# A Conformer and gMLP layer on one core: every third low half of the weights on GpSimd

## The chip, the cores and the metric

The kernel runs on one core of a Trainium2 chip. The metric is the time of one execution on the device in microseconds (us). The engines are named as in the profile: PE is TensorE (matmuls), DVE is VectorE, ACT is ScalarE, POOL is GpSimd, SP issues most of the DMAs. Each engine works through its own list of instructions in order, and semaphores make one wait for another.

## The reference

One layer works on 512 tokens of 1024 channels, in float32:

```python
h = h + 0.5 * swiglu(rms_norm(h, ffn1_norm), ffn1_w_gu, ffn1_w_down)      # 1024 -> 2 x 2816 -> 1024
n = rms_norm(h, mix_norm)
a_val, a_gate, b_u, b_v, g_a, g_b = split(n @ w_in + b_in, 6)             # 1024 -> 6 x 1024
y_a = silu(layer_norm(causal_depthwise_conv(a_val * sigmoid(a_gate)))) @ w_a_out   # width 31
y_b = (gelu(b_u) * spatial_mix(layer_norm(gelu(b_v)))) @ w_b_out          # chunks of 128 tokens
h = h + (sigmoid(g_a) * y_a + sigmoid(g_b) * y_b) @ w_out
h = h + memory_cross_attention(rms_norm(h), rms_norm(mem), w_q, w_kv, w_o)  # 4 heads, 256 tokens
h = h + 0.5 * swiglu(rms_norm(h, ffn2_norm), ffn2_w_gu, ffn2_w_down)
y = rms_norm(h, final_norm)
```

## The kernel before

The activations lie transposed, channels on 128 partitions and the 512 tokens along the free axis, in eight tiles. Every large product is done in three passes of TensorE on numbers split in two: the high half is the number rounded to the engine's fast float32 form (fp32r), the low half what is left. `mm3` adds high x high, high x low and low x high into one PSUM tile.

Weights come in blocks of up to 128 x 1024 numbers. `wfetch` loads a block (four buffers, DMAs issued by SP), `wsplit` makes its halves: ScalarE writes the high half (`whi`, line 96), VectorE subtracts it from the raw block and writes the low half (`wlo`, line 97); each half has three buffers. A block then feeds 24 matmuls of 512 columns. A block's split can start only when the buffers of the block three before it have been read by TensorE.

The stages are: the first feed-forward (pairs `g`, `u`, then `d`), keys of the memory (`pk`), the input projection (`av`, `ag`, then `r` with tokens on partitions, then `gb`), the branch B product (`yb`), gates A (`ga`), values (`pv`), branch A (`ya`), the output product (`o`), attention (`pq`, `wo`), and the second feed-forward. The name of a low half in the profile is that of its product, the first K tile of the block and an l: `gb0w0l`.

The convolution is vector work: 240 steps (line 344), each multiplies a shifted channel tile by a weight and adds it. They run at any time after their channel tile exists and are written as generators; `spend` issues some of them behind each block of weights, by assumed lengths (a split 1.14 us, a K tile's matmuls 0.65 us). When all of a tile's steps are done it is added to `csum` (line 348), whose mean is a matmul, `pmean` (line 501). On top of this order of writing, the framework's scheduler sets the final list of each engine: it runs a model of the engines' timeline and picks, among the instructions that are ready there, by the order of writing. So a change of one instruction's engine changes the lists of all engines.

GpSimd has little to do: constants at the start, the powers -1/2 of the norms (`pow_mhalf`, line 196), one mask (line 369), and the issue of the loads of a few rows (lines 366 and 376). VectorE's other work in the convolution's stretch are evictions of `r` (line 387, from PSUM), the layer norm of branch B (lines 401 to 413) and halves of activations (line 180).

Of the kernel before, what the change touches and what calls it, by code (L numbers as in the profile page):

```python
# [10 lines left out]
F32 = mybir.dt.float32  # L11
F32R = mybir.dt.float32r
AF = mybir.ActivationFunctionType
ALU = mybir.AluOpType
# [11 lines left out]
CW = 31  # L26
# [6 lines left out]

# lengths that the order of issue goes by: a K tile's products of 512 columns, a block's split, a vector operation
MM_US, SPLIT_US, OP_US = 0.65, 1.14, 0.66
# [12 lines left out]
def conformer_layer(ctx: ExitStack, tc: tile.TileContext, xT, memT, vecs, rows, w_gu1, w_dn1, w_in_f, w_in_t,  # L48
# [33 lines left out]
    def wfetch(srcs, name):  # L82
        """the blocks [128, K tiles, 128 or 512 columns] one after the other in one tile"""
        raw = wpool.tile([P, 1024], F32, tag="raw", name=name, bufs=4)
        n = 0
        for src in srcs:
            m = src.shape[1] * src.shape[2]
            nc.sync.dma_start(out=raw[:, n:n + m], in_=src.rearrange("p k c -> p (k c)"))
            n += m
        return raw[:, :n]  # L90

    def wsplit(raw, c, name):
        n = raw.shape[1]
        hi = wpool.tile([P, 1024], F32R, tag="whi", name=name + "h", bufs=3)[:, :n]
        lo = wpool.tile([P, 1024], F32R, tag="wlo", name=name + "l", bufs=3)[:, :n]
        S.copy(out=hi, in_=raw)  # L96
        V.tensor_tensor(out=lo, in0=raw, in1=hi.bitcast(F32), op=ALU.subtract)  # L97
        return hi.rearrange("p (k c) -> p k c", c=c), lo.rearrange("p (k c) -> p k c", c=c)
# [8 lines left out]

    # steps of vector work that may run at any time (generators that give each step's length) stand behind the
    # blocks of weights, as many as the products of a block leave room for; soon: in order, first; later: by turns
    soon, later = deque(), deque()  # L110
    room = [None]

    def spend(us):
        """vector work us long has been issued; positive room is filled with steps"""
        if room[0] is not None:
            room[0] = min(room[0], 4.0) - us
            while (soon or later) and room[0] > 0:
                steps = soon or later
                used = next(steps[0], None)
                if used is None:  # L120
                    steps.popleft()
                    continue
                room[0] -= used
                if steps is later and len(steps) > 1:
                    steps[0], steps[1] = steps[1], steps[0]
# [9 lines left out]
    def part(acc, wsrc, ahi, alo, k0, k1, name):  # L135
        """K tiles k0 to k1 of a product with wsrc [128, K tiles, 128 columns] stationary, activations moving."""
        nk = wsrc.shape[1]
        whi, wlo = wload(wsrc[:, k0:k1, :], f"{name}w{k0}")
        for k in range(k0, k1):
            mm3(acc, whi[:, k - k0, :], wlo[:, k - k0, :], ahi[k], alo[k], k == 0, k == nk - 1)  # L140
        spend(SPLIT_US - MM_US * (k1 - k0) * acc.shape[1] / T)

    def linear(wsrc, ahi, alo, name, n=T):
        """a whole product: PSUM tile [128 columns, n]"""
        nk = wsrc.shape[1]
        acc = new_ps(name)[:, :n]
        for k0 in range(0, nk, 8):
            part(acc, wsrc, ahi, alo, k0, min(nk, k0 + 8), name)
        return acc

    def linear_pair(wsrcs, ahi, alo, name):
        """two products side by side, K tile by K tile, for activations that come one by one"""
        accs = [new_ps(f"{name}{i}") for i in range(2)]
        for k0 in range(0, DT, DT // 2):
            ks = slice(k0, k0 + DT // 2)
            whi, wlo = wsplit(wfetch([w[:, ks, :] for w in wsrcs], f"{name}w{k0}"), P, f"{name}w{k0}")
            for k in range(k0, k0 + DT // 2):
                for i in range(2):
                    c = i * DT // 2 + k - k0
                    mm3(accs[i], whi[:, c, :], wlo[:, c, :], ahi[k], alo[k], k == 0, k == DT - 1)  # L160
        return accs

    def linear_rows(wsrc, ahi, alo, ntok, name):
        """activations stationary, wsrc [128, K tiles, 512 columns] moving: PSUM tiles [128 tokens, 512]."""
        nk = wsrc.shape[1]
# [33 lines left out]
    def rstat(accs, n, eps, name, copy=True):  # L199
        """accs [128, n]: per partition sums of squares. 1/sqrt(mean + eps) as columns [128 tokens, n/128] and as  # L200
        rows on all partitions [128, n]."""
        nt = n // P
# [21 lines left out]
    def prep(m, g, acc):  # L224
        """residual tile m is final: operands of the next product and its part of the norm."""
        split_x(m, g)
        add_square(acc, h[:, m, :], m == 0)
# [23 lines left out]
    def ffn_up(w_gu, rb, first=()):  # L251
        """the hidden activations, split; first: products of the first pairs that are already there"""
        f = [gate_up(pg, pu, rb, j) for j, (pg, pu) in enumerate(first)]
# [8 lines left out]

    # the first two pairs of products go along with the loads, K tile by K tile
    HF = DT // 2
# [70 lines left out]
    def conv(i):  # L335
        """causal depthwise convolution of a channel tile; tap k reaches CW - 1 - k tokens back"""
        c = slot(f"cv{i}")
# [12 lines left out]

    # gated channels
    room[0] = 0
# [10 lines left out]

    # spatial gating unit, tokens on partitions
    wsr = slot("wsr")
    nc.gpsimd.dma_start(out=wsr, in_=sgu_wT.rearrange("s g t -> s (g t)"))
    # [s, t]: kept where t >= s
    wsr3 = wsr.rearrange("s (g t) -> s g t", g=GROUPS)
# [10 lines left out]
    def token_major(which):  # L379
        """gelu of 1024 columns of the input projection: tiles [token tile][column half]"""  # L380
        out = [[None, None] for _ in range(TT)]
# [68 lines left out]

    # the rest of the keys and the values of the memory, and the steps of the spatial gating in between
    vts = [[None, None], [None, None]]
# [30 lines left out]

    # sigmoid(gate_B) * y_B
    for m in range(DT):
# [12 lines left out]

    # layer norm over channels, swish
    pmean = ps2.tile([P, T], F32, tag="st", name="pmean")  # L500
# [24 lines left out]

    # sigmoid(gate_A) * y_A, merge
    mgh, mgl = [], []
# [44 lines left out]
    def softmax(hd):  # L572
        """probabilities [128 tokens, memory], two token tiles side by side"""
        out = []
# [53 lines left out]

    # independent products stand between the steps of a head
    q = {}  # L630
# [28 lines left out]
    for m in range(last):  # L659
        add_half(m, linear(w_dn2[m], fh, fl, f"d{m}"))  # L660
        add_square(acc, h[:, m, :], m == 0)
        S.activation(h[:, m, :], h[:, m, :], AF.Copy, scale=col("final_norm", m))
    # the last product and the final norm by halves of the tokens
    ws = [wload(w_dn2[last][:, k0:min(FT, k0 + 8), :], f"dl{k0}") for k0 in range(0, FT, 8)]
# [76 lines left out]
```

## Time and profile before

| | us |
|---|---|
| time, median of 3 runs (lowest, highest) | 1356.83 (1355.51, 1357.62) |
| span of the profiled execution | 1355.1 |
| PE busy | 1332.3 |
| DVE busy | 777.9 |
| ACT busy | 456.5 |
| POOL busy | 19.4 |

The profile is of one execution; its span runs from the first instruction to the last, and its whole time is not given apart from the span. Busy time is the time in which an engine has an instruction at work. Instructions of one engine overlap a little at their ends: a matmul of 512 columns is recorded with 0.40 us though the next starts 0.23 us later, and two VectorE operations overlap by some 0.08 us. The start and end of GpSimd's instructions are rough.

### The profile page before, as it was taken

How to read it: one execution, taken by the hardware profiler on the slowest of the kernel's cores; microseconds unless marked ns; L12 is line 12 of the kernel's file. 1: busy time of each engine (PE TensorE's matmuls, PEld its weight loads, DVE VectorE, ACT ScalarE, POOL GpSimd, SP SyncE). 2: the span in 40 equal slices, each digit the busy share in tenths (PEclk: the TensorE clock that was granted, in tenths of full speed). 3: DMA queues.
4: the chain of work that ended last, by engine and by line, in shares of the span. 5: the costliest groups of instructions: out<-in, count | busy, mean ns of one | idle time of the engine just before them, and what ended most of it. 6: DMA issues, size and time to landing. Idle time of an engine off the chain costs nothing.

```text
span 1355.1 us, 14923 instructions
## 1 busy us (share of the span) xinstructions
PE 1332.3 (98%) x5968; PEld 1079.1 (80%) x5968; DVE 777.9 (57%) x1078; ACT 456.5 (34%) x618; POOL 19.4 (1%) x31
## 2 busy tenths in 40 slices
PE   7999999999999999999999999999999999999996
PEld 6788888888898888888787788887878888888886
DVE  5544444434367999998996775554644444442323
ACT  5322222223233223343224743334432222222221
POOL 0000000000020000100000000000000000000000
PEclk9999999999999999999999999999999999999998
DMA  6333333233353332322233333202332333323321
GB/s 207 109 94 93 94 93 94 86 96 109 114 181 115 94 94 94 101 97 76 92 94 116 102 109 109 62 20 76 123 93 93 94 94 93 94 86 101 86 70 62
DMA packets 40660, 132.47 MB, mean 98 GB/s; under 512 B 4432, under 2 KB 7248, under 8 KB 40592
## 3 DMA queue, kind: packets, MB, share of 16 engines
q1 hardware_dynamic: 39872, 129.17, 30.9%
q0 software_dynamic: 720, 2.36, 0.6%
q8 instruction: 46, 0.75, 0.2%
q14 instruction: 22, 0.18, 0.0%
HBM read 129.42 MB, written 2.10 MB: 97 GB/s over the span
## 4 chain that ended last, share of the span: by engine, by line
PE 97%; DVE 1%; ACT 1%; DMA 0%; issue 0%; SPq 0%; DVEq 0%; POOLq 0%; ACTq 0%
PE u L106 6%; PE g L104 6%; PE u L105 6%; PE g L105 6%; PE g L106 6%; PE u L104 6%; PE d L106 6%; PE d L104 6%; PE d L105 6%; PE r L173 2%; PE r L172 2%; PE r L174 2%; PE ya L104 1%; PE ya L105 1%; PE o L105 1%; PE av L105 1%
## 5 line engine op out<-in xcount | busy, mean ns | idle before, releaser
L344 DVE SCALAR_TENSOR_TENSOR cv<-ap,vec,cv 128x494 f32<-128x494 f32 (+24 forms) x240 | 163.3, 729 | 0.4
L244 DVE TENSOR_TENSOR u<-u,n4rb 128x512 f32<-128x512 f32 x22 | 15.2, 692 | 70.3 <-PE u L106 70.3
L244 DVE TENSOR_TENSOR u<-u,n1rb 128x512 f32<-128x512 f32 x20 | 13.8, 691 | 65.8 <-PE u L106 65.8
L240 DVE TENSOR_TENSOR g<-g,n4rb 128x512 f32<-128x512 f32 x22 | 15.2, 692 | 51.7 <-PE g L106 47.5
L240 DVE TENSOR_TENSOR g<-g,n1rb 128x512 f32<-128x512 f32 x20 | 13.8, 691 | 43.3 <-PE g L106 43.3
L246 DVE TENSOR_TENSOR f<-s,u 128x512 f32<-128x512 f32 x44 | 30.4, 692 | 5.4 <-ACT s L242 1.1
L261 DVE SCALAR_TENSOR_TENSOR h<-d,h 128x512 f32<-128x512 f32 x15 | 10.4, 692 | 31.5 <-PE d L106 31.5
L242 ACT ACTIVATE s<-g 128x512 f32<-128x512 f32 x44 | 27.8, 633 | 0.1
L192 DVE TENSOR_TENSOR acc<-acc,sq 128x512 f32<-128x512 f32 x34 | 23.3, 685 | 0.1
L191 ACT ACTIVATE sq<-h 128x512 f32<-128x512 f32 x34 | 21.2, 624 | 1.4 <-DVE h L261 0.2
L184 DVE SCALAR_TENSOR_TENSOR xlo<-h,vec,xhi 128x512 fp32r<-128x512 f32 x24 | 17.7, 746 | 5.3 <-ACT xhi L183 5.2
L183 ACT ACTIVATE xhi<-h,vec 128x512 fp32r<-128x512 f32 x24 | 17.2, 717 | 1.9 <-DVE h L626 1.0
L543 DVE TENSOR_TENSOR h<-o,h 128x512 f32<-128x512 f32 x8 | 5.5, 692 | 13.7 <-PE o L106 13.7
L532 DVE TENSOR_TENSOR ga<-ya,sga 128x512 f32<-128x512 f32 x8 | 5.5, 690 | 13.4 <-PE ya L106 13.4
L387 DVE TENSOR_TENSOR uv<-r,br 128x512 f32<-128x512 f32 x16 | 10.7, 686 | 0.1
L104 PE MATMUL fg<-xhi,first0h 128*128 128x512 f32 x4 | 2.2, 553 | 7.8 <-ACT first0h L96 7.8
L587 ACT ACTIVATE pr<-sc,mx 128x256 f32<-128x256 f32 x16 | 7.4, 470 | 6.4 <-DVE mx L584 6.3
L567 DVE TENSOR_TENSOR qt<-pq,n3rb 128x512 f32<-128x512 f32 x8 | 5.3, 687 | 7.3 <-ACT n3rb L218 4.3
L626 DVE TENSOR_TENSOR h<-wo,h 128x512 f32<-128x512 f32 x8 | 5.4, 688 | 7.0 <-PE wo L106 7.0
L388 ACT ACTIVATE uv<-uv 128x512 f32<-128x512 f32 x16 | 9.0, 621 | 0.6 <-DVE uv L387 0.6
L583 DVE TENSOR_REDUCE mx<-sc 128x2 f32<-128x512 f32 x8 | 5.5, 692 | 3.7 <-PE sc L106 3.3
L97 DVE TENSOR_TENSOR d1w8l<-d1w,d1w8h 128x1024 fp32r<-128x1024 f32 x2 | 2.5, 1226 | 8.7 <-ACT d1w8h L96 8.7
(4300 smaller groups left out, 4279.4 us busy)
## 6 DMA issues: line engine op xcount, KB each, us to landing
h<-xT SPq DMA_DIRECT2D x8, 256.0 KB, 5.9
first<-w_gu SPq DMA_DIRECT2D x8, 256.0 KB, 6.1
d0w<-w_dn SPq DMA_DIRECT2D x4, 512.0 KB, 3.5
d1w<-w_dn SPq DMA_DIRECT2D x4, 512.0 KB, 3.7
d2w<-w_dn SPq DMA_DIRECT2D x4, 512.0 KB, 3.4
d3w<-w_dn SPq DMA_DIRECT2D x4, 512.0 KB, 3.5
d4w<-w_dn SPq DMA_DIRECT2D x4, 512.0 KB, 3.6
d5w<-w_dn SPq DMA_DIRECT2D x4, 512.0 KB, 3.4
```

Of the source, the lines that this page charges most:

```text
L104: PE.matmul(out, whi, ahi, start=start, stop=False)
L105: PE.matmul(out, whi, alo, start=False, stop=False)
L106: PE.matmul(out, wlo, ahi, start=False, stop=stop)
L172: PE.matmul(accs[t], a_h, whi[:, k - k0, :], start=k == 0, stop=False)
L173: PE.matmul(accs[t], a_h, wlo[:, k - k0, :], start=False, stop=False)
L174: PE.matmul(accs[t], a_l, whi[:, k - k0, :], start=False, stop=k == nk - 1)
L192: V.tensor_tensor(out=acc, in0=acc, in1=sq, op=ALU.add)
L240: V.tensor_tensor(out=g1, in0=pg, in1=rb, op=ALU.mult)
L242: S.activation(s1, g1, AF.Silu)
L244: V.tensor_tensor(out=u1, in0=pu, in1=rb, op=ALU.mult)
L246: V.tensor_tensor(out=f, in0=s1, in1=u1, op=ALU.mult)
L344: V.scalar_tensor_tensor(out=o, in0=aps[i][:, :T - back], scalar=w, in1=o, op0=ALU.mult, op1=ALU.add)
```

## The change

Every third call of `wsplit` gives the subtract to GpSimd instead of VectorE. The rest of the diff removes comments and blank lines, with no effect on the program; lines from 95 on stand three further down.

```diff
+    turn = [0]
+
     def wsplit(raw, c, name):
         n = raw.shape[1]
         hi = wpool.tile([P, 1024], F32R, tag="whi", name=name + "h", bufs=3)[:, :n]
         lo = wpool.tile([P, 1024], F32R, tag="wlo", name=name + "l", bufs=3)[:, :n]
         S.copy(out=hi, in_=raw)
-        V.tensor_tensor(out=lo, in0=raw, in1=hi.bitcast(F32), op=ALU.subtract)
+        turn[0] += 1
+        (G if turn[0] % 3 == 0 else V).tensor_tensor(out=lo, in0=raw, in1=hi.bitcast(F32), op=ALU.subtract)
```

GpSimd's list, from the second norm's power (n2r) to the loads of the rows for the `r` products. Before:

```order
L196 TENSOR_TENSOR nmr<-nmm,mhalf 128x2
L196 TENSOR_TENSOR n2r<-n2m,mhalf 128x4
L366 DMA wsr<-sgu_wT 128x512
L369 AFFINE_SELECT wsr<-wsr 128x512
L376 DMA br_3436<-rows 128x512
L376 DMA br_3599<-rows 128x512
```

The same place in the changed kernel:

```order
L199 TENSOR_TENSOR n2r<-n2m,mhalf 128x4
L100 TENSOR_TENSOR av0w0l<-av0w_2809,av0w0h 128x1024
L100 TENSOR_TENSOR ag1w0l<-ag1w_2920,ag1w0h 128x1024
L100 TENSOR_TENSOR av3w0l<-av3w_3040,av3w0h 128x1024
L100 TENSOR_TENSOR ag4w0l<-ag4w_3155,ag4w0h 128x1024
L100 TENSOR_TENSOR av6w0l<-av6w_3273,av6w0h 128x1024
L100 TENSOR_TENSOR ag7w0l<-ag7w_3387,ag7w0h 128x1024
L100 TENSOR_TENSOR r10w4l<-r10w_3513,r10w4h 128x1024
L369 DMA wsr<-sgu_wT 128x512
L372 AFFINE_SELECT wsr<-wsr 128x512
L379 DMA br_3436<-rows 128x512
L100 TENSOR_TENSOR r11w2l<-r11w_3637,r11w2h 128x1024
```

The loads of the mask's weights and of the bias rows, which stood right behind n2r, now stand behind seven subtracts and more.

VectorE's list where it comes to the low half gb0w0l (cv are convolution steps; the columns tell how far each channel tile has come, a smaller number being a later step). Before:

```order
L97 TENSOR_TENSOR pk7w0l<-pk7w_4164,pk7w0h 128x1024
L344 SCALAR_TENSOR_TENSOR cv_3418<-ap_3114,vec,cv_3418 128x492
L344 SCALAR_TENSOR_TENSOR cv_3583<-ap_3193,vec,cv_3583 128x493
L387 TENSOR_TENSOR uv_4101<-r_3948,br_3946 128x512
L344 SCALAR_TENSOR_TENSOR cv_4095<-ap_3270,vec,cv_4095 128x508
L387 TENSOR_TENSOR uv_4104<-r_3949,br_3946 128x512
L387 TENSOR_TENSOR uv_4107<-r_3950,br_3946 128x512
L387 TENSOR_TENSOR uv_4110<-r_3951,br_3946 128x512
L344 SCALAR_TENSOR_TENSOR cv_3418<-ap_3114,vec,cv_3418 128x491
L344 SCALAR_TENSOR_TENSOR cv_3583<-ap_3193,vec,cv_3583 128x492
L97 TENSOR_TENSOR gb0w0l<-gb0w_4209,gb0w0h 128x1024
```

The same place in the changed kernel:

```order
L347 SCALAR_TENSOR_TENSOR cv_4095<-ap_3270,vec,cv_4095 128x507
L347 SCALAR_TENSOR_TENSOR cv_3583<-ap_3193,vec,cv_3583 128x487
L390 TENSOR_TENSOR uv_4101<-r_3948,br_3946 128x512
L347 SCALAR_TENSOR_TENSOR cv_3418<-ap_3114,vec,cv_3418 128x482
L390 TENSOR_TENSOR uv_4104<-r_3949,br_3946 128x512
L347 SCALAR_TENSOR_TENSOR cv_4095<-ap_3270,vec,cv_4095 128x506
L390 TENSOR_TENSOR uv_4107<-r_3950,br_3946 128x512
L347 SCALAR_TENSOR_TENSOR cv_3583<-ap_3193,vec,cv_3583 128x486
L390 TENSOR_TENSOR uv_4110<-r_3951,br_3946 128x512
L351 TENSOR_TENSOR csum<-csum,cv_3418 128x512
L100 TENSOR_TENSOR gb0w0l<-gb0w_4209,gb0w0h 128x1024
```

pk7w0l has gone to GpSimd, and by gb0w0l the channel tile cv_3418 has come to its last step (482 columns) and its csum, where it stood at 491 before. From av2w0l to gb0w0l VectorE's list held 30 low halves, 135 convolution steps and 2 csum before, and holds 20, 152 and 3 now. From gb0w0l to the last csum it held 21 low halves, 105 steps and 5 csum, and holds 13, 88 and 4. In TensorE's list pmean stands 62 matmuls earlier than before, and near av2 the order of two blocks is changed: before, the block ag1 is read in one piece ahead of av2's low half; now TensorE reads av2w0l first, where it read ag1w0l, and ag1w0l seven matmuls later.

## Rows read from the trace of the kernel before

**Rows 1.** The page's first part: busy us (share of the span) xinstructions.
```profile
span 1355.1 us, 14923 instructions
...
PE 1332.3 (98%) x5968; PEld 1079.1 (80%) x5968; DVE 777.9 (57%) x1078; ACT 456.5 (34%) x618; POOL 19.4 (1%) x31
```

**Rows 2.** Waits of PE: waiting, released by, us in total, times, longest.
```profile
PE fg L104 <- ACT first0h L96: 7.8, 1, 7.8
...
PE po L104 <- ACT ph L179: 2.3, 4, 0.6
...
PE ya L104 <- ACT aa0h L179: 1.3, 1, 1.3
PE yb L104 <- ACT yb5w0h L96: 0.2, 1, 0.2
```

**Rows 3.** Busy us by stretch, each with its number of instructions, and the clock.
```profile
core 0: us, PE busy (x) PEld busy (x) DVE busy (x) ACT busy (x) POOL busy (x), PEclk, DMA share, GB/s
50.00:380.00 330.00, 330.00 (x1416) 265.49 (x1415) 137.00 (x167) 95.61 (x123) 0.00 (x0) 1.00 0.32 97
419.40:584.10 164.70, 164.70 (x724) 133.19 (x723) 156.26 (x225) 50.78 (x62) 4.27 (x5) 1.00 0.32 101
584.10:708.70 124.60, 124.01 (x578) 100.57 (x578) 117.75 (x173) 39.81 (x54) 0.00 (x0) 1.00 0.29 93
```

**Rows 4.** Timeline of DVE: start us, us, engine line op out<-in xcount, idle before.
```profile
649.70 6.56 DVE L344 SCALAR_TENSOR_TENSOR cv<-ap,vec,cv 128x488 f32<-128x488 f32 x10
...
661.05 1.22 DVE L97 TENSOR_TENSOR yb4w0l<-yb4w,yb4w0h 128x1024 fp32r<-128x1024 f32 x1
662.18 1.22 DVE L97 TENSOR_TENSOR yb5w0l<-yb5w,yb5w0h 128x1024 fp32r<-128x1024 f32 x1
```

**Rows 5.** Timeline of POOL.
```profile
1.37 0.29 POOL masks.py:199 TENSOR_SCALAR_AFFINE_SELECT ident<-ident 128x128 f32<-128x128 f32 x1
...
389.22 2.07 POOL L196 TENSOR_TENSOR n2r<-n2m,mhalf 128x4 f32<-128x4 f32 x1 [6.02 <-DVE n2m L208]
...
395.20 0.64 POOL L369 TENSOR_SCALAR_AFFINE_SELECT wsr<-wsr 128x512 f32<-128x512 f32 x1 [3.23 <-DMA wsr<-sgu_wT]
...
857.69 1.01 POOL L196 TENSOR_TENSOR n3r<-n3m,mhalf 128x4 f32<-128x4 f32 x1 [121.64 <-DVE n3m L208]
```

**Rows 6.** DVE beside them; then line 329: ns min/median/max, first and last start.
```profile
389.20 1.23 DVE L97 TENSOR_TENSOR pk4w0l<-pk4w,pk4w0h 128x1024 fp32r<-128x1024 f32 x1
...
395.40 0.98 DVE L329 SCALAR_TENSOR_TENSOR xn<-h,vec,n2rb 128x512 f32<-128x512 f32 x1 [1.29 <-ACT n2rb L218]
...
L329 DVE SCALAR_TENSOR_TENSOR xn<-h,vec,n2rb x8: 737/741/981, 395.4 to 407.7; 128x512 f32<-128x512 f32 x8
```

**Rows 7.** Timelines of ACT, DVE and PE at the blocks ag1 and av2.
```profile
415.94 1.05 ACT L96 CAST ag1w0h<-ag1w 128x1024 fp32r<-128x1024 f32 x1 [6.85 <-PE av L105]
416.90 1.05 ACT L96 CAST av2w0h<-av2w 128x1024 fp32r<-128x1024 f32 x1
...
418.17 1.22 DVE L97 TENSOR_TENSOR av2w0l<-av2w,av2w0h 128x1024 fp32r<-128x1024 f32 x1
...
418.73 0.40 PE L106 MATMUL ag<-xhi,ag1w0l 128*128 128x512 f32 x1
```

**Rows 8.** Timelines of DVE and PE at gb0.
```profile
582.86 1.22 DVE L97 TENSOR_TENSOR gb0w0l<-gb0w,gb0w0h 128x1024 fp32r<-128x1024 f32 x1
...
587.04 0.40 PE L106 MATMUL gb<-xhi,gb0w0l 128*128 128x512 f32 x1
```

**Rows 9.** Timelines of DVE and PE at the last csum and at pmean.
```profile
708.00 0.69 DVE L348 TENSOR_TENSOR csum<-csum,cv 128x512 f32<-128x512 f32 x1
...
713.76 1.02 PE L501 MATMUL pmean<-csum,avg 128*128 128x512 f32 x2
```

**Rows 10.** Timelines of DVE and PE at a block of the first feed-forward.
```profile
47.42 1.22 DVE L97 TENSOR_TENSOR g4w0l<-g4w,g4w0h 128x1024 fp32r<-128x1024 f32 x1
...
57.14 0.40 PE L106 MATMUL g<-xhi,g4w0l 128*128 128x512 f32 x1
```

## The prediction

> **What bounds the kernel now.** I read the page's first part, then the waits of TensorE, then the busy time of the engines by stretch, and last the timelines of VectorE and GpSimd in the stretch where VectorE is full. The reader is to see first that TensorE is busy for 1332.3 of 1355.1 us, VectorE for 777.9 and GpSimd for 19.4 [rows 1]. Of TensorE's idle time 7.8 us lie at the start and the rest mostly at the end; the waits in between are a few us in all, such as 2.3 us for the softmax's halves and 1.3 us for the first normed channel tile [rows 2]. So a shorter VectorE can bring almost nothing, 4 us at most: 22.8 us of idle less the start and some 11 us of the end. What can go wrong is that TensorE starts to wait.
>
> VectorE's share of 57% is an average over two kinds of stage. In the feed-forward from 50 to 380 us it works 137.0 of 330 us; between 419.4 and 584.1 us it works 156.26 of 164.70, because the steps of the convolution are issued there, and from there to 708.7 us 117.75 of 124.60 [rows 3]. [...] The change is decided where VectorE has 8 us to spare in 165.
>
> **The change part by part.** Removed from VectorE: each third subtract of a block. Two of them back to back start 1.13 us apart, so one costs 1.13 us, and a step of the convolution 0.655 us (ten in 6.56) [rows 4]. Added to GpSimd: the same subtract there, which no row of before shows. Moved: the scheduler knows of the lighter VectorE and pulls convolution steps forward.
>
> In the feed-forward nothing should follow. A low half is finished at 48.64 us and TensorE first reads it at 57.14, a lead of 8.5 us [rows 10]; GpSimd may take 3 us instead of 1.2 and still be early, and VectorE has more than half its time free.
>
> *How long GpSimd holds VectorE up.* GpSimd's one-input operation takes 0.29 us on 128 columns and 0.64 on 512 [rows 5], that is 0.91 ns an element. Two inputs read one after the other over 1024 columns would be 1.87 us, both at once 0.93.
> Are the two engines independent? Two places say no. The small power operation n2r takes 2.07 us where it starts 0.02 us behind VectorE's pk4w0l, and n3r, of the same form and with VectorE idle, 1.01 [rows 5, 6]: n2r got its inputs when pk4w0l ended (390.43 us) and was done 0.86 us later. In the other direction, the first L329 starts at 395.40 us, while the select on 512 columns runs on GpSimd from 395.20 to 395.84; it takes 0.98 us, and its seven sisters 0.74 [rows 5, 6]. It was held 0.24 us, up to 0.2 us before the end of GpSimd's instruction. So the two shut each other out, and the shut-out lasts about as long as GpSimd reads.
> [...]
> The ends from rows alone: 0.93 us (both inputs at once), and 2.9 us (1.87 of reading and the 1.01 of a four-column operation, all of it held). I take 1.9 us, nearest to the held L329, where the hold was over just before the instruction ended.
>
> *The stretch to gb0.* I count between the end of av2w0l on VectorE and the end of gb0w0l (in VectorE's list). Ten subtracts go to GpSimd (av3, ag4, av6, ag7, r10w4, r11w2, r00w0, r00w6, r01w4, pk7): 10 x 1.13 = 11.3 us less. But 152 convolution steps stand there now, not 135: 17 x 0.655 = 11.1 us more, and one more csum, 0.6. So 156.3 - 11.3 + 11.1 + 0.6 = 156.7 us of VectorE's own work: the relief has been spent already by the order. On top come the ten holds, 10 x 1.9 = 19 us: 175.7 us in a stretch of 164.7. It is 11.0 us late, and the idle 8.4 us of before are used up in that sum.
> At the head of the stretch av2w0l itself is later. ag1w0l's cast ends at 416.99 us and it runs on GpSimd from there; av2w0l's cast ends at 417.95, so it waits until 416.99 + 1.9 = 418.9 and ends at 420.1 instead of 419.4: 0.7 us. TensorE wants it at 418.7 in the new order, where it wanted ag1w0l [rows 7]: a wait of 1.4 us, which is part of the total and not beside it, since both engines shift.
> At the end gb0w0l ended at 584.08 and was first read at 587.04, a lead of 3.0 us [rows 8]. So TensorE has lost 0.7 + 11.0 - 3.0 = 8.7 us by then. Of VectorE's 232 rows there, 28 read one SBUF tensor or almost nothing and are not held, 12%: 19 x 0.12 = 2.3 us less. That leaves 6.4 us.
>
> *Behind gb0.* VectorE's 117.75 us to the last csum lose 17 convolution steps, eight L97 and a csum (11.1 + 9.0 + 0.6) and gain six holds (11.4): 108.5 us. From 584.1 + 0.7 + 11.0 = 595.8 us it would be done at 704.3 without idle time. pmean, which reads csum, stood at 713.76 [rows 9] and stands 62 matmuls earlier in TensorE's list now; at 330 us / 1416 = 0.233 us each [rows 3] that is 14.5 us, so 699.3 and, with 8.7 us lost, 708.0. There are 3.7 us left, so I count no new wait.
> In the projections after it (ya) and the attention, a held VectorE loses 1.9 - 1.13 = 0.8 us for each of the few subtracts on GpSimd that fall between the steps of a chain. TensorE waits there already [rows 2]. pmean's earlier place gives ya room; I count one such delay in attention, 0.8 us.
>
> GpSimd's own queue: the loads of the bias and norm rows now stand behind r10w4l, r11w2l and r00w0l, and the power operations of the layer norm behind r00w6l. What waits behind such a subtract waits some 2 to 3 us; the rows are wanted at evictions that are a block of 5.6 us or more (24 x 0.233) away. I count nothing; if one decided, it would be up to 3 us, once.
>
> **Sum.** 6.4 + 0.8 = 7.2 us. The profiled execution's span is 1355.1 us, of which the runs' times (1355.51 to 1357.62) leave 0.4 to 2.5 us around it; the change touches nothing there. 1356.8 + 7.2 = 1364.0 us.
>
> **The rivals.**
> *The hold is short.* If GpSimd takes both inputs at once (0.93 us), the stretch needs 156.7 + 9.3 = 166.0 us against 164.7 + 3.0: no loss by gb0, only 0.7 us at av2w0l, which is not delayed then but wanted earlier (419.4 against 418.7). 1357.5 us, no change. For it: the hold on L329 was only 0.24 us, and the reading rate is got from two short instructions. Against it: it needs the two inputs not to share what one input fills.
> *The hold is the whole instruction.* At 2.9 us av2w0l is 1.7 us late, and 1.7 + 156.7 + 29 - 167.7 = 19.7 us, less 12% of 29, so 16.2; from 584.1 + 1.7 + 21.0 = 606.8 us the rest (97.1 + 6 x 2.9) ends at 721.3, 2 us behind pmean's 699.3 + 19.7: 18 us, 1375 us. For it: n2r needed 0.86 us after its release for four columns. Against it: L329 went on before the select had ended.
> *The other side: VectorE is relieved and nothing holds it.* One mechanism, in the convolution stage: with no hold, VectorE has 156.7 us of work in 164.7, and TensorE's waits on late splits go (yb3 to yb5, ya, the attention's halves). The price is bounded by the 4 us of waits; I would expect 0.5 to 2 us, 1355 to 1356 us. It decides if a hold costs less than the 1.13 us that a subtract frees. For it: VectorE is short of time from 440 to 708 us. Against it: the order has spent the relief, and the two rows show a hold.
> *GpSimd is late with its own halves.* It would need more than 8.5 us in the feed-forward [rows 10]; nothing in the rows comes near.
>
> **How the numbers follow.** The forecast (holds of 1.6 to 2.4 us, 1361 to 1369 us) has 0.56; the long hold 0.12; the short hold 0.22, a quarter of it above the bound; the relief 0.10, a third of it beyond the bound. A measurement of this kernel tells 0.2%, 2.7 us, from no change: its three runs spread over 2.1. So slower 0.56 + 0.12 + 0.05 = 0.73, within 0.2% 0.17 + 0.07 = 0.24, faster 0.03; for what I have not seen I move some of the first to the others: 0.69, 0.25 and 0.06. The range takes in the short hold and most of the long one: 1355.8 to 1375.
>
> **What would show it.** Right: convolution steps of 0.73 us that now and then last 2 to 2.6 us, each while GpSimd subtracts; GpSimd's subtracts of 2 to 3 us; VectorE over 97% busy from 420 to 590 us; TensorE idle for 5 to 10 us there, released by VectorE's low halves (r01, gb0, gb1), with at most a few us elsewhere; the feed-forward as before. Wrong: convolution steps that stay at 0.73 us beside a running subtract, TensorE waiting for GpSimd's halves rather than VectorE's, a loss that lies in the attention or at pmean, or a granted clock below 1.00 in the middle.

## The result, and the profile after

| | us |
|---|---|
| time after, median of 3 runs (lowest, highest) | 1363.91 (1362.80, 1364.22) |
| time before | 1356.83 |
| ratio, 95% interval | 1.0051 [1.0031, 1.0070] |
| span of the profiled execution after (before) | 1362.0 (1355.1) |

The change makes the kernel 7.1 us slower; 1364.0 was forecast. The page's first part, as [rows 1] of before:

```profile
span 1362.0 us, 14902 instructions
...
PE 1333.4 (98%) x5968; PEld 1078.4 (79%) x5968; DVE 762.6 (56%) x997; ACT 458.3 (34%) x618; POOL 241.4 (18%) x112
```

GpSimd has 81 subtracts and 222 us more. VectorE has 81 instructions less, which at 1.13 us would be 91 us, but it is busy for only 15 us less. What it was given back it has lost: the convolution steps (L344 before, L347 now) in the page's costliest groups took 163.3 us before, 729 ns each, and now:

```profile
L347 DVE SCALAR_TENSOR_TENSOR cv<-ap,vec,cv 128x503 f32<-128x503 f32 (+28 forms) x240 | 195.5, 857 | 1.1
```

These are 32 of the 76 us lost. Another 36 us lie in the halves of activations (lines 180 and 184 of before), all outside the convolution's stretch.

The waits of TensorE, without those that stand unchanged in [rows 2]:

```profile
PE r L176 <- DVE r01w2l L100: 1.5, 1, 1.5
...
PE pk L107 <- DVE uv L390: 1.0, 1, 1.0
PE pm L107 <- ACT vh L182: 1.0, 2, 0.7
PE wo L109 <- POOL wo4w0l L100: 0.6, 1, 0.6
PE r L175 <- DVE uv L390: 0.6, 2, 0.4
PE r L176 <- DVE r01w0l L100: 0.6, 1, 0.6
PE av L109 <- DVE av2w0l L100: 0.6, 1, 0.6
```

No wait is long; nearly all end with something that VectorE is late with, directly (low halves, the evictions uv) or through ScalarE (vh is made from an eviction). Only one, 0.6 us, ends with GpSimd's own low half. The busy time by stretch, in the columns of [rows 3]:

```profile
50.00:380.00 330.00, 330.00 (x1416) 265.47 (x1415) 125.61 (x150) 96.50 (x125) 50.44 (x20) 1.00 0.31 98
...
419.50:595.10 175.60, 170.39 (x746) 135.90 (x746) 174.65 (x233) 54.12 (x66) 55.75 (x24) 1.00 0.33 107
595.10:704.00 108.90, 108.90 (x506) 89.27 (x507) 108.05 (x146) 32.96 (x43) 17.46 (x6) 1.00 0.29 92
```

In the feed-forward TensorE is busy throughout, as before. In the stretch from av2w0l to gb0w0l VectorE is now busy for 174.65 of 175.60 us, and TensorE has 5.2 us idle where it had none. After that TensorE does not wait again up to 704 us. The clock is 1.00 in all three, so no part of the loss is the clock's.

Now the holds themselves. VectorE's timeline around two of GpSimd's subtracts and at gb0 (columns as in [rows 4]):

```profile
447.83 1.23 DVE L100 TENSOR_TENSOR av5w0l<-av5w,av5w0h 128x1024 fp32r<-128x1024 f32 x1
448.96 2.88 DVE L347 SCALAR_TENSOR_TENSOR cv<-ap,vec,cv 128x491 f32<-128x491 f32 x1
...
475.46 7.16 DVE L347 SCALAR_TENSOR_TENSOR cv<-ap,vec,cv 128x482 f32<-128x482 f32 x11
482.54 1.22 DVE L100 TENSOR_TENSOR r10w0l<-r10w,r10w0h 128x1024 fp32r<-128x1024 f32 x1
483.67 2.86 DVE L347 SCALAR_TENSOR_TENSOR cv<-ap,vec,cv 128x486 f32<-128x486 f32 x1
...
593.79 1.22 DVE L100 TENSOR_TENSOR gb0w0l<-gb0w,gb0w0h 128x1024 fp32r<-128x1024 f32 x1
```

GpSimd's timeline, one subtract that had nothing to wait for and the two that belong to the held steps above:

```profile
416.01 2.41 POOL L100 TENSOR_TENSOR ag1w0l<-ag1w,ag1w0h 128x1024 fp32r<-128x1024 f32 x1 [17.41 <-PE ag L108]
...
442.27 9.05 POOL L100 TENSOR_TENSOR ag4w0l<-ag4w,ag4w0h 128x1024 fp32r<-128x1024 f32 x1 [12.29 <-ACT ag4w0h L98]
...
475.87 10.15 POOL L100 TENSOR_TENSOR ag7w0l<-ag7w,ag7w0h 128x1024 fp32r<-128x1024 f32 x1 [11.53 <-ACT ag7w0h L98]
```

A subtract takes GpSimd 2.41 us. Each holds one VectorE instruction: a step that lasts 0.73 us lasts 2.86 or 2.88 beside it, so it is held 2.15 us. From av2w0l to gb0w0l the instructions that are longer than the same form was before exceed it by 19.4 us together, 19.05 of it beside the ten subtracts (the shortest hold is 1.0 us, seven are 2.13 to 2.16) and 0.4 beside the mask's select. TensorE's timeline shows the outcome at both ends of the stretch and at ag7, to be read beside [rows 7, 8]:

```profile
419.55 0.50 PE L109 MATMUL av<-xhi,av2w0l 128*128 128x512 f32 x1 [0.55 <-DVE av2w0l L100]
...
486.39 0.40 PE L109 MATMUL ag<-xhi,ag7w0l 128*128 128x512 f32 x1
...
595.06 0.50 PE L109 MATMUL gb<-xhi,gb0w0l 128*128 128x512 f32 x1
```

gb0w0l is first read at 595.06 us, 8.0 us later than before, 0.05 us after VectorE has finished it (595.01): the lead of 3.0 us is gone. The rest of the program follows it, 7.0 us late at the output product.

### The profile page after: what moved, and what is told of

The parts are those of the page before. It is cut to its first block, busy times and chain, and to the rows that moved or that the text cites. A ratio compares the mean times of both kernels' runs of the same rounds, so it can differ in the third digit from the quotient of the medians.

```text
span 1362.0 us, 14902 instructions
## 1 busy us (share of the span) xinstructions
PE 1333.4 (98%) x5968; PEld 1078.4 (79%) x5968; DVE 762.6 (56%) x997; ACT 458.3 (34%) x618; POOL 241.4 (18%) x112
## 4 chain that ended last, share of the span: by engine, by line
PE 84%; DVE 12%; issue 2%; ACT 1%; DMA 0%; POOL 0%; SPq 0%; DVEq 0%; POOLq 0%; ACTq 0%
DVE cv L347 8%; PE g L107 6%; PE u L107 6%; PE u L109 6%; PE g L109 6%; PE g L108 6%; PE u L108 6%; PE d L107 6%; PE d L108 6%; PE d L109 6%; PE ya L107 1%; PE ya L108 1%; PE gb L109 1%; PE ga L107 1%; PE o L109 1%
## 5 line engine op out<-in xcount | busy, mean ns | idle before, releaser
L347 DVE SCALAR_TENSOR_TENSOR cv<-ap,vec,cv 128x503 f32<-128x503 f32 (+28 forms) x240 | 195.5, 857 | 1.1
L187 DVE SCALAR_TENSOR_TENSOR xlo<-h,vec,xhi 128x512 fp32r<-128x512 f32 x24 | 26.9, 1126 | 9.4 <-ACT xhi L186 9.3
L186 ACT ACTIVATE xhi<-h,vec 128x512 fp32r<-128x512 f32 x24 | 17.2, 716 | 1.1 <-DVE h L629 0.9
L100 POOL TENSOR_TENSOR ag7w0l<-ag7w,ag7w0h 128x1024 fp32r<-128x1024 f32 x1 | 10.2, 10152 | 11.5 <-ACT ag7w0h L98 11.5
L100 POOL TENSOR_TENSOR ag4w0l<-ag4w,ag4w0h 128x1024 fp32r<-128x1024 f32 x1 | 9.1, 9051 | 12.3 <-ACT ag4w0h L98 12.3
L390 DVE TENSOR_TENSOR uv<-r,br 128x512 f32<-128x512 f32 x16 | 10.8, 680 | 0.0
```

The lines of the kernel that those rows point to most:

```text
L100: (G if turn[0] % 3 == 0 else V).tensor_tensor(out=lo, in0=raw, in1=hi.bitcast(F32), op=ALU.subtract)
L187: V.scalar_tensor_tensor(out=lo, in0=src, scalar=g, in1=hi.bitcast(F32), op0=ALU.mult, op1=ALU.subtract)
L347: V.scalar_tensor_tensor(out=o, in0=aps[i][:, :T - back], scalar=w, in1=o, op0=ALU.mult, op1=ALU.add)
```

## The experiments

The theory: GpSimd's reads shut VectorE out, which costs TensorE something only where VectorE is full, in one stretch, after 8.4 us of idle time and 3.0 us of lead are used up. The rivals: each hold costs its share wherever it falls; the new order is what costs, not the reads; the hold has another size or another cause. "Holds" below are summed as above, from the end of av2w0l to gb0w0l; "gb0" is how much later than before TensorE first reads gb0w0l, in one profiled execution of each. These executions differ by up to 2.0 us already in the first feed-forward; the table at the end gives this beside it.

**Only in the middle, and only outside.** Two kernels: GpSimd gets its third either only in the stage with the convolution (av to the end of its steps), or only outside it.

```diff
-        (G if turn[0] % 3 == 0 else V).tensor_tensor(...)
+        (G if turn[0] % 3 == 0 and room[0] is not None else V).tensor_tensor(...)   # inside
+        (G if turn[0] % 3 == 0 and room[0] is None else V).tensor_tensor(...)       # outside
```

> GpSimd takes each third low half only while convolution steps are being issued (av to yb, 17 blocks); all other low halves stay on VectorE. Theory (GpSimd's reads hold VectorE in the convolution's stretch, and that is all): the whole loss is here, 1362 to 1365 us, with ten long VectorE steps of about 2 us excess each at most before gb0. Rival (the loss is made by all 80 subtracts, also in attention and feed-forward): less than half of the 7.1 us, 1358 to 1360 us.

> The reverse: GpSimd takes each third low half only outside that part (both feed-forwards, ga, ya, attention), VectorE all others. Theory: 1356 to 1358 us, no change that can be told from before, though GpSimd's subtracts still take 2.4 us and still hold VectorE there: TensorE has 8 us of lead. Rival (subtracts in attention and in the chain of the norms cost too): 1359 us or more.

Beside 1356.49 us of the kernel before, inside took 1363.34 us, ratio 1.0054 [1.0039, 1.0069], and outside 1357.04, ratio 1.0006 [0.9997, 1.0015]. The busy row of the stretch, inside:

```profile
419.50:595.10 175.60, 170.08 (x745) 135.87 (x745) 174.65 (x233) 54.07 (x67) 55.68 (x24) 1.00 0.33 107
```

It is the row of the changed kernel, and VectorE's list in the stretch is the same, instruction for instruction. The whole loss lies in the stage of the convolution, with 17 of the 81 blocks there; the other 64 cost nothing that can be measured, though TensorE waits there for two of GpSimd's own halves (0.7 us for wo4w0l, 0.4 for pv1w2l).

**GpSimd writes only.** GpSimd sets each third low half to 0 instead of subtracting, so that this part of the products is left out. From av2w0l to gb0w0l VectorE has the same instructions as in the changed kernel, but from the ninth on in another order; the expectation took the lists to be the same.

```diff
-        (G if turn[0] % 3 == 0 else V).tensor_tensor(out=lo, in0=raw, in1=hi.bitcast(F32), op=ALU.subtract)
+        if turn[0] % 3 == 0:
+            G.memset(lo.bitcast(F32), 0.0)
+        else:
+            V.tensor_tensor(out=lo, in0=raw, in1=hi.bitcast(F32), op=ALU.subtract)
```

> As the changed kernel, but GpSimd fills each third low half with zeros instead of subtracting: the low half's part of those products is left out. It reads nothing; VectorE's list up to gb0 is that of the changed kernel (20 low halves, 152 convolution steps). Theory (the hold comes from GpSimd's reads): no long convolution steps, VectorE needs 156.7 us in 164.7, so the loss is gone: 1354.5 to 1357.5 us. Rival (the other order of the lists costs the 7 us, not the hold): 1362 to 1365 us.

1353.73 us, ratio 0.9985 [0.9975, 0.9994]: the loss is gone and 2.7 us are gained, 0.8 more than the best that was expected. GpSimd's timeline, then the durations of all convolution steps (ns, min/median/max), then the busy row of the stretch:

```profile
439.08 0.96 POOL L101 MEMSET ag4w0l<- 128x1024 f32 x1 [15.84 <-PE av L112]
```

```profile
L350 DVE SCALAR_TENSOR_TENSOR cv<-ap,vec,cv x240: 673/728/751, 419.7 to 688.0; 128x488 f32<-128x488 f32 x6, 128x486 f32<-128x486 f32 x6, 128x484 f32<-128x484 f32 x6, 128x491 f32<-128x491 f32 x6
```

```profile
419.40:584.10 164.70, 164.70 (x730) 133.46 (x729) 156.03 (x234) 50.51 (x62) 18.32 (x24) 1.00 0.36 109
```

The longest of 240 steps is 0.751 us: GpSimd's memsets of 0.96 us, which only write, hold no step. So the reads hold, and pulling the steps forward costs nothing by itself. The exact order of the changed kernel was not run without reads; that it costs nothing is argued from the sum (the holds fill VectorE's stretch), not shown. VectorE's 156.03 us are the 156.26 of [rows 3]: ten subtracts less, the steps pulled forward in their place.

**The reads without the relief.** VectorE keeps all low halves; GpSimd subtracts each third block of the middle stage a second time, into a tile that nobody reads.

```diff
+    turn = [0]
...
         V.tensor_tensor(out=lo, in0=raw, in1=hi.bitcast(F32), op=ALU.subtract)
+        turn[0] += 1
+        if turn[0] % 3 == 0 and room[0] is not None:
+            junk = big.tile([P, 1024], mybir.dt.bfloat16, tag="s", name="junk", bufs=50)[:, :n]
+            G.tensor_tensor(out=junk, in0=raw, in1=hi.bitcast(F32), op=ALU.subtract)
```

> The kernel before, VectorE does every low half in the old order (30 low halves, 135 convolution steps up to gb0), and GpSimd does each third subtract of the convolution stage once more into a tile that nobody reads. Theory: ten holds of 1.9 us on 156.3 us of work in a stretch of 164.7 with a lead of 3.0: 156.3 + 19 - 167.7 = 7.6 us of loss, 1362 to 1367 us. Rival (reordering): no loss, 1356 to 1358 us, since nothing of VectorE's list has moved.

1370.77 us, ratio 1.0110 [1.0095, 1.0125], +14.3 us: the direction was right, the size too small. Two of TensorE's waits:

```profile
PE r L179 <- DVE r10w4l L99: 3.5, 1, 3.5
PE ya L110 <- ACT aa0h L185: 3.5, 1, 3.5
```

Holds 19.2 us, gb0 10.1 us late. av2w0l ends 3.8 us later than before, since it is held itself by 2.2 us and TensorE had waited 1.3 us at av0 for a half of the activations; from there to the end of gb0w0l it takes 9.3 us longer; and the lead of 3.0 us is gone. VectorE's list has as many low halves, steps and csum up to gb0 as before, but from r10w4l on not in the same order. Before, and then in this run, the steps between r10w2l and r10w4l, and the held av2w0l:

```profile
487.19 3.93 DVE L344 SCALAR_TENSOR_TENSOR cv<-ap,vec,cv 128x498 f32<-128x498 f32 x6
```

```profile
419.76 3.43 DVE L99 TENSOR_TENSOR av2w0l<-av2w,av2w0h 128x1024 fp32r<-128x1024 f32 x1
...
494.99 8.40 DVE L350 SCALAR_TENSOR_TENSOR cv<-ap,vec,cv 128x498 f32<-128x498 f32 x13
```

So TensorE's wait for r10w4l comes from the new order as well as from the holds, and this run does not refute the rival. The other 4 us come behind gb0, where VectorE has kept all its low halves as well: TensorE waits 3.5 us for the first normed channel tile, 1.3 before [rows 2], and its clock falls. Right after each of the two waits of 3.5 us the granted clock is 0.50; it is 1.00 in the middle of the changed kernel. The second place and the stretch behind it, in the columns of [rows 3]:

```profile
770.78:774.19 3.41, 3.32 (x9) 2.11 (x8) 3.28 (x6) 3.41 (x7) 0.00 (x0) 0.50 0.66 243
774.19:777.60 3.41, 3.41 (x17) 2.73 (x16) 2.15 (x4) 3.38 (x7) 0.00 (x0) 1.00 0.02 8
```

Nine matmuls instead of seventeen are some 1.7 us of these 4, an estimate. My expectation had stopped at gb0.

**One operand instead of two.** The same, but GpSimd only copies the raw block to the spare tile.

```diff
-            G.tensor_tensor(out=junk, in0=raw, in1=hi.bitcast(F32), op=ALU.subtract)
+            G.tensor_copy(out=junk, in_=raw)
```

> The lists of the kernel before; GpSimd copies the raw block of every third block of the middle stage into a tile nobody reads: one operand read instead of two. Theory (VectorE is held for as long as GpSimd reads, and one operand takes about half the reads): holds of about 1 us, ten of them 10 us, which do not fill what TensorE leaves: 1356 to 1360 us. Rival A (VectorE is held for the whole instruction whatever it reads): holds of 2 us as with the doubled subtract, 1367 to 1371 us. Rival B (a copy of one operand holds nothing): no VectorE instruction longer than before, 1356 to 1357 us.

1357.02 us beside 1356.28, ratio 1.0006 [0.9996, 1.0015]; holds 5.9 us, gb0 not late (here too VectorE's order changes, from the mask's half wsl on). GpSimd's copy and the two steps beside it, which take 1.39 us where nothing holds them:

```profile
442.24 1.04 POOL L103 CAST junk<-av6w 128x1024 bf16<-128x1024 f32 x1 [14.43 <-DMA av6w<-w_in_f]
```

```profile
442.28 2.18 DVE L350 SCALAR_TENSOR_TENSOR cv<-ap,vec,cv 128x504 f32<-128x504 f32 x2
```

The hold is 0.79 us. One operand holds too, so rival B falls by the trace, though its time is the same. But the run doesn't separate the theory from rival A: the copy itself lasts 1.04 us, not 2.4, and I had given rival A the longer one. Hold and instruction differ by 0.25 us here (1.04 and 0.79) as with the subtract (2.40 and 2.15): both read, and GpSimd shuts VectorE out for all but 0.25 us of them.

**Four pieces.** The changed kernel, each subtract of GpSimd cut in four.

```diff
-        (G if turn[0] % 3 == 0 else V).tensor_tensor(out=lo, in0=raw, in1=hi.bitcast(F32), op=ALU.subtract)
+        if turn[0] % 3 == 0:
+            q = n // 4
+            for p in range(0, n, q):
+                G.tensor_tensor(out=lo[:, p:p + q], in0=raw[:, p:p + q], in1=hi[:, p:p + q].bitcast(F32), op=ALU.subtract)
+        else:
+            V.tensor_tensor(out=lo, in0=raw, in1=hi.bitcast(F32), op=ALU.subtract)
```

> The changed kernel, but GpSimd subtracts in four pieces of 256 columns. Theory (the hold is by element): four holds of about 0.5 us in place of one of 2, the same sum, so 1362 to 1365 us, and TensorE is late at gb0 as with one piece. Rival A (the hold has a fixed part for each instruction): more than 2.5 us for a block, 1367 us or more, with the delay still behind VectorE's gb0w0l. Rival B (GpSimd has to wait for a pause in VectorE's run each time, as it waited 7 us at ag4w0l and ag7w0l): its low halves come up to 4 times 7 us late, more than their lead of 10 to 20 us, and TensorE waits for GpSimd's halves themselves: 1375 us or more.

1358.65 us, ratio 1.0019 [1.0009, 1.0028]: below what any of the three said. VectorE and GpSimd at r00w0:

```profile
525.90 1.22 DVE L105 TENSOR_TENSOR r11w6l<-r11w,r11w6h 128x1024 fp32r<-128x1024 f32 x1
527.04 5.28 DVE L352 SCALAR_TENSOR_TENSOR cv<-ap,vec,cv 128x504 f32<-128x504 f32 x5
```

```profile
526.29 4.84 POOL L103 TENSOR_TENSOR r00w0l<-r00w,r00w0h 128x256 fp32r<-128x256 f32 x4 [12.13 <-ACT r00w0h L98]
```

Four of the five steps last 1.21 or 1.22 us instead of 0.73: held 0.48 us each, 1.9 for the block against 2.15 in one piece. A piece alone takes GpSimd 0.74 us, so the 0.25 us that do not count are now there four times. And some pieces meet an instruction that isn't held: of the four beside av3 only three held anything, 1.24 us in all. Holds 15.4 us instead of 19.4, gb0 4.4 us late instead of 8.0, or 3.8 instead of 8.5 counted from the feed-forward: 4.7 us less, as the time falls by 5. Not all of it is the smaller holds. The lists have changed here too: TensorE reads ag1w0l ahead of av2w0l again and loses nothing there, where the changed kernel loses 1.4 us up to av3w0l. My "same sum" was wrong, since each piece leaves 0.25 us free and small pieces fit beside what isn't held.

**Every sixth and every second block.** `% 6` and `% 2` in place of `% 3`.

> GpSimd gets the low half of every sixth block instead of every third. Theory (a sum in one stretch against a lead): between av2w0l and gb0w0l VectorE has 143 convolution steps and 25 low halves in place of 152 and 20, and about 5 holds of 1.9 us: its own work and the holds are about 165.4 us, where TensorE leaves it 164.7 and the low half of gb0 had been 3.0 us early. So the time is that of the kernel before: 1356.5 to 1358 us, ratio 0.999 to 1.001. Rival (each hold costs its share, wherever it falls): half of the +7 us, 1360 to 1361 us.

> GpSimd gets the low half of every second block. Theory: 157 convolution steps and 15 low halves on VectorE and 15 holds of 1.9 us in the same stretch: about 15 us past what TensorE leaves, so 1370 to 1376 us, more than twice the loss of every third block. Rival (each hold costs its share): 1.5 times +7 us, 1367 to 1368 us.

Every sixth: 1357.74 us, ratio 1.0014 [1.0005, 1.0023], within the theory's time and a little over its ratio. Every second: 1376.78 us, ratio 1.0152 [1.0135, 1.0169], 0.8 us above the theory's upper end and 9 above the rival's. Half of the subtracts cost 1.5 us, all of them 7, one and a half times as many 20.5. So the loss isn't a share for each hold: it sets in when the idle time is used up. With every second block the holds are 28.4 us and gb0 is 17.2 us late; three of TensorE's waits there:

```profile
PE pmean L504 <- DVE csum L351: 2.3, 1, 2.3
...
PE ag L109 <- POOL ag0w0l L100: 0.5, 1, 0.5
PE ag L109 <- POOL ag4w0l L100: 0.4, 1, 0.4
```

Here csum is late for pmean and GpSimd for its own halves, two steps that I counted at nothing for every third. As in the doubled subtract the granted clock is 0.50 right after long waits, of 3.9, 5.0 and 2.3 us. The last of them is the one for pmean, behind gb0:

```profile
715.08:718.49 3.41, 3.41 (x9) 2.65 (x9) 2.75 (x5) 1.67 (x3) 0.00 (x0) 0.50 0.48 191
718.49:721.90 3.41, 3.41 (x16) 2.73 (x16) 3.41 (x6) 3.41 (x7) 0.00 (x0) 1.00 0.00 0
```

So some 4 of the 20.5 us, an estimate, are this wait and the slow matmuls behind it, which the theory had not counted. In the two places before gb0 VectorE is full, and what the clock costs there was not separated. The other kernels show no such fall between the start and the end.

The loss with every sixth has one place. VectorE's timeline, and the wait of TensorE:

```profile
418.42 2.62 DVE L100 TENSOR_TENSOR av2w0l<-av2w,av2w0h 128x1024 fp32r<-128x1024 f32 x1 [7.97 <-ACT av2w0h L98]
```

```profile
PE av L109 <- DVE av2w0l L100: 1.8, 1, 1.8
```

VectorE has been idle for 8 us there, but av2w0l is wanted at once, and GpSimd reads ag1's block from 417.57 to 419.95. TensorE waits 1.8 us for it; 1.4 of this are the hold (2.62 us instead of 1.22), though VectorE isn't full.

**The other sixths.** `% 6 == 3`: every sixth block again, but ag1 stays with VectorE; then the same in four pieces.

> Every sixth block again, but the other ones: av0, av3, av6, r10w4 in place of ag1, ag4, ag7, r11w2. Theory: the +1.4 us of every sixth block was one event, VectorE's av2w0l held while GpSimd subtracted ag1w0l (TensorE waited 1.8 us there); with ag1 left to VectorE this wait goes. Between av2w0l and gb0w0l there are 145 steps, 25 low halves and five holds of 1.9 us: 166.7 us against 167.7, so no wait at gb0 either: 1355.5 to 1357.3 us. Rival (a hold costs its share wherever it falls): 1357.5 to 1358.5 us again, with TensorE waiting at other low halves.

> As the run before it, each GpSimd subtract in four pieces of 256 columns. Theory: five blocks with holds of about 1.5 us in place of 1.9 leave gb0w0l 2 us earlier, but TensorE does not wait there in either: 1355 to 1357.3 us, no difference from the run before it that can be told; at best a part of the 2.7 us of the run in which GpSimd only wrote. Rival: the relief of VectorE counts as soon as holds are small, so 1353.5 to 1355 us, faster than both kernels.

Beside 1356.35 us of before: 1355.69 us, ratio 0.9996 [0.9987, 1.0005], and 1355.54 us, ratio 0.9993 [0.9984, 1.0002]. Both as the theory has it; neither is faster than before by more than the measurement is uncertain. Holds 9.4 and 7.3 us, TensorE at gb0 0.6 and 0.5 us earlier than before; since these executions were 1.2 and 0.5 us ahead in the feed-forward, that is 0.5 us lost and nothing. Of TensorE's waits in the stretch none is over 0.2 us. The head without GpSimd, VectorE and then TensorE:

```profile
415.23 1.22 DVE L100 TENSOR_TENSOR ag1w0l<-ag1w,ag1w0h 128x1024 fp32r<-128x1024 f32 x1 [5.38 <-ACT ag1w0h L98]
416.40 1.22 DVE L100 TENSOR_TENSOR av2w0l<-av2w,av2w0h 128x1024 fp32r<-128x1024 f32 x1
```

```profile
418.10 0.40 PE L109 MATMUL ag<-xhi,ag1w0l 128*128 128x512 f32 x1
```

Both halves are ready before TensorE comes to the first. With the same share of blocks, which ones are moved made a difference of 2 us. TensorE's order differs as well: with ag1 moved it reads av2w0l first, here ag1w0l. So the two together are shown, not the hold alone.

The kernels in one table, by holds. The last column but one tells how much later than before TensorE is in the first feed-forward, where the change costs nothing; what is lost up to gb0 is the column before it less this one.

| GpSimd | holds, us | av2w0l itself held, us | gb0 late, us | late in the first feed-forward, us | time less that of before, us |
|---|---|---|---|---|---|
| every second | 28.4 | 1.2 | 17.2 | -0.7 | +20.5 |
| third (the change) | 19.4 | 1.1 | 8.0 | -0.5 | +7.1 |
| third, done twice | 19.2 | 2.2 | 10.1 | -0.1 | +14.3 |
| third, in four pieces | 15.4 | 0.3 | 4.4 | 0.6 | +2.4 |
| sixth, without ag1 | 9.4 | 0 | -0.6 | -1.2 | -0.7 |
| third, copied once more | 5.9 | 0 | -0.8 | -0.4 | +0.7 |
| sixth, with ag1 | 5.1 | 1.4 | 2.0 | 0.5 | +1.5 |

Two rows don't follow the order. The last one loses its time at av2. The doubled subtract has the holds of the changed kernel and loses twice as much: 1.8 us more up to gb0, where its av2w0l is later, and the rest behind gb0, where VectorE has all its low halves to do. That giving the subtracts away helps behind gb0 is likely but not shown, since the order and the clock differ as well.

## Why the prediction was right

*Where it is decided.* Right. TensorE idles between 419 and 595 us and nowhere else by more than 0.6 us above before; the feed-forward does not notice [rows 10], and GpSimd's subtracts take 2.4 to 2.8 us there, under the 3 us allowed for.

*The hold.* The kind was right, the size too small. 1.9 us was taken, 2.15 measured where a subtract falls fully beside held instructions. As at L329 the hold ends a little before GpSimd's instruction, here 0.26 us; what was too small is the reading time, 1.87 us, worked out from two short selects. The subtract takes 2.41 us, and 0.74 on 256 columns: 2.17 ns a column, where twice 0.91 was taken. The cause, reading, is shown by the run that only writes, where no step lasts longer than 0.751 us.

*The discount.* 12%, 2.3 us, was right in size: ten full holds would be 21.5 us, and the ten add up to 19.05, since three are partly covered: 1.0 us at av3w0l, 1.5 at av6w0l and at r00w6l. That is 11% less. Beside the start of these subtracts stand L362, which reads one operand from PSUM (0.75 and 0.74 us), and L404, which reads one tensor (0.69 us), none longer than before (0.75 and 0.69 at most); at av3w0l VectorE was idle for 0.67 us before it too. That such an instruction isn't held stood in no row of before; the trace of the changed kernel shows it for these two forms. But the discount, taken off holds of 1.9 us, left 16.7. That ten holds of 1.9 without the discount come to the measured sum is chance.

*The relief is spent by the order.* Shown: 156.03 us of VectorE's own work in the run that only writes, 156.7 forecast. From the end of av2w0l to the end of gb0w0l VectorE took 175.5 us (419.49 to 595.01), where the forecast less its discount was 173.4.

*The head, the lead and the sum.* The execution after the change was 0.5 us ahead already in the first feed-forward, to be read beside [rows 10]:

```profile
56.66 0.40 PE L109 MATMUL g<-xhi,g4w0l 128*128 128x512 f32 x1
```

Executions differ by that much. Counted from there, av2w0l on VectorE ended 0.6 us later than before (0.7 forecast), the stretch took 10.8 us longer, and the lead of 3.0 us was used up: TensorE has lost 8.5 us at gb0, where 6.4 was forecast. The 2.1 us between them are the size of the hold, less 0.7 us of VectorE's own work that was counted too much. What followed brought the forecast out right: 1.0 us was regained from gb0 to the yb blocks, where nothing was counted, and 0.5 lost at wo4, where 0.8 was. That makes 8.0 us. The profiled execution was 0.5 us ahead at the start and makes up another 0.7 at its end, where executions differ too (0.6 in the copied run, none in the run inside), so the spans differ by 6.8, as TensorE's first reads in the two traces show. The mechanism and the size to 2 us are the prediction's; that it met the 7.1 us of the times to 0.1 is luck.

*Behind gb0.* No new wait up to pmean, as forecast; it was close. VectorE's last csum and TensorE's pmean:

```profile
704.20 0.69 DVE L351 TENSOR_TENSOR csum<-csum,cv 128x512 f32<-128x512 f32 x1
```

```profile
706.36 1.02 PE L504 MATMUL pmean<-csum,avg 128*128 128x512 f32 x2
```

1.5 us were left (3.7 forecast), and with every second block it became a wait.

*GpSimd's own queue.* The loads that stand behind its subtracts were counted at nothing; from 480 to 600 us the trace shows no wait of VectorE for anything, so none of them was late.

*Attention.* One delay of 0.8 us was counted for VectorE held there; it is 0.6 us, of which 0.2 were there before, and for another reason: TensorE waits for GpSimd's own wo4w0l, which takes 2.4 us instead of VectorE's 1.2.

*The rivals.* The short hold is refuted by the hold's size, 2.15 us. Of the whole instruction only the length, 2.9 us, is: nearly the whole of GpSimd's 2.41 us does hold. The relief is there, 2.7 us in the run that only writes (0.5 to 2 expected), though GpSimd's own part is shorter there too (0.96 us) and needs no high half; up to gb0 it has no chance beside the reads. *GpSimd late with its own halves* was dismissed from a lead in the feed-forward, which was the wrong place to look: at ag7 GpSimd was done at 486.02 us and TensorE read at 486.39, 0.4 us from a wait, and with every second block the wait came.

## What to carry to other kernels

In these runs GpSimd's subtracts and copies of 1024 columns, which read SBUF, held VectorE's convolution steps and low halves, which read two SBUF tensors each: beside a subtract of 2.41 us a step was held 2.15, beside a copy of 1.04 us 0.79. Count such work as VectorE time of nearly its full length on GpSimd, 2.15 us here for a subtract that cost VectorE 1.13. Ask next whether VectorE is full in that stage, taking its idle time and its lead together: below this the holds cost nothing here (9.4 us of holds, 0.7 us less than before), above it further holds turned into delay (19.4 us of holds, 7.1 us more; 28.4 us, 20.5 more), and a scheduler that knows nothing of the holds fills the place that was freed. A hold on an instruction that is wanted at once costs also where VectorE has been idle: 1.4 us at av2w0l with every sixth block, after 8 us of idle time. And long waits of TensorE can cost more than their length: right after waits of 2.3 to 5.0 us its granted clock was 0.50 in two of the runs, for 3.41 us in the two places shown, and 1.00 behind that.

## What the runs showed of the hardware that was not expected

GpSimd can wait long for its turn. ag7w0l starts at 475.87 us and ends at 486.02, 10.15 us for a 2.4 us subtract, while eleven convolution steps (475.46 to 482.62, back to back, none longer than 0.74 us) and a low half go by; only the step behind the low half is held. ag4w0l waits in the same way (9.05 us), and with every second block one took 11.0. The two exclude each other here, but the second's turn does not come when the first has finished: GpSimd was passed over eleven times. In the changed kernel the long waits end behind a low half (ag4w0l, ag7w0l) or behind L362, which reads one operand from PSUM (av6w0l, 5.27 us); elsewhere (r10w4l at 492.67 us) GpSimd got in between two convolution steps. What decides this was not tested and stays open. In four pieces, the first piece of ag7w0l took 8.5 us and the others 0.7 to 1.2 each; so a piece that comes right behind another mostly does not wait anew.
